# Thirty-one stores of a hybrid decoder layer issued from ScalarE's queue in place of SP's

## The chip, the cores and the metric

The kernel runs on one core of a Trainium2 chip. The core has five engines that run side by side, each with its own queue of instructions, executed in order: TensorE (PE: matrix products; PEld is its loading of weights), VectorE (DVE), ScalarE (ACT), GpSimd (POOL) and SyncE (SP), which only issues transfers. Transfers (DMAs) move data between the chip's memory and the on-chip buffers; sixteen DMA engines carry them out after some engine's queue has issued them. The metric is the time of one execution on the device in microseconds (us). Three runs of the kernel before gave 1281.14, 1285.14 and 1290.57 us; the median is 1285.14.

## What is computed

One layer of a decoder with two token mixers over 1024 tokens of width 1024. In float32, cut to what matters:

```python
h = rmsnorm(x, norm_w) * (1 + scale) + shift          # shift, scale, gate from c
z_ssm, xbc, dt_raw, q, k, v, z_att, f_logit, g_logit = split(h @ w_in)
y_ssm = ssd_branch(z_ssm, xbc, dt_raw, ...)           # conv, chunked scan (16 heads, chunks of 128)
y_att = fox_branch(q, k, v, z_att, f_logit, b_f)      # causal attention, 8 heads, forget gates
g_ssm, g_att = split(sigmoid(g_logit + b_gate))
merged = g_ssm * (y_ssm @ w_proj_ssm) + g_att * (y_att @ w_proj_att)
out = rmsnorm(x + gate * (merged @ w_out), final_norm_w)
```

## The kernel before

Every product is made of three passes of a reduced-precision matrix product: each operand is split into a high part (a cast on ScalarE, line 102) and a low part (a subtraction on GpSimd or VectorE, line 103). Weights come in as pieces of 128 x 512 floats into one of four raw buffers (`wr`, loaded at lines 89, 462 and 579), and are split into `wh` and `wl`. A raw buffer is free again once its low part has been made.

The stages follow each other in the code:

- To about 160 us: adaLN, the normalised and transposed input `hh`/`hl`, the first three gate slabs, the first V slab (`v_slab(0)`, narrow matmuls at lines 140 to 142, which also gives dt and the forget logits), sums of the input for the pair products (`t_forms`, lines 440 to 444), and the chain for dt (lines 369 to 396).
- To about 545 us: the pairs of slabs (`c_pair`, matmuls at lines 495 to 497), each pair of the projection's 128-column slabs by seven products instead of eight. Each slab's result is evacuated into a buffer of the ring `ev` (four buffers of 128 x 1028 floats) and stored to DRAM scratch: gates (line 187), z (526), the convolved x (545). Between them stand sums of later weights (lines 579 to 594).
- To about 770 us: the scan (`ssd_half`, 32 chunk steps of four heads). Each step loads `ab` from a_scr (line 681), makes the decay matrix on ScalarE (683, 685), VectorE (686) and the split (`m`), transposes x (691), updates the carried state (711 to 717) and makes the outputs (728, 739 and 740, 741 to 744). To keep TensorE busy, three V slabs (lines 140 to 142) and seven slabs of q and k (lines 115 to 117, `qk_spill`) are put among the steps as fill; V is stored at line 350, q and k at line 194.
- To about 1070 us attention by heads, which reads V, q and k back; then the rest of the output products.

All transfers are issued from SP's queue. The order of each queue is not the order of the code: a scheduler of the framework places every instruction of the whole program by the durations that it assumes and by priorities (the scan's steps have a higher one than the fill). A store waits on its queue until the engine that writes its source has finished; what stands behind it on that queue waits with it. Eight semaphores go round for the completion of transfers: a transfer also waits for the one that last used its semaphore, which is the eighth before it.

The stores in question are made by `gate_out` (16 gates), `qk_out` (7 slabs of q and k) and the evacuation of `v_slab` (two stores for each of four slabs), each of 512 KB. In all three the data are written by ScalarE: a tanh (186), a scaled copy (193), a copy (346).

Of the kernel before, what the change touches and what calls it, by code (L numbers as in the profile page):

```python
# [32 lines left out]
S = 1024  # L33
# [36 lines left out]
def build(ctx, tc, t):  # L70
    nc = tc.nc
    V, A, G, PE, SP = nc.vector, nc.scalar, nc.gpsimd, nc.tensor, nc.sync
# [10 lines left out]
    def ev(name):  # L83
        return evp.tile([P, 1028], F32, tag="ev", bufs=4, name=name)
# [42 lines left out]
    def t_slab(srcs, n, xh, xl, evac, per=None):  # L127

        us = [unit(s, 2 * n) for s in srcs]
        per = per or 512 // n  # L130
        st = 512 // per
        for tb0 in range(0, 8, per):
            ps = mm_tile()
            for i in range(per):
                ts = slice((tb0 + i) * P, (tb0 + i + 1) * P)
                o = ps[:, i * st:i * st + n]
                for k in range(8):
                    hi, lo = us[k // 2]
                    cs = slice((k % 2) * n, (k % 2 + 1) * n)
                    PE.matmul(o, lhsT=xh[k][:, ts], rhs=hi[:, cs], start=(k == 0), stop=False)  # L140
                    PE.matmul(o, lhsT=xh[k][:, ts], rhs=lo[:, cs], start=False, stop=False)  # L141
                    PE.matmul(o, lhsT=xl[k][:, ts], rhs=hi[:, cs], start=False, stop=(k == 7))  # L142
            evac(tb0, ps.rearrange("p (i c) -> p i c", i=per))
# [21 lines left out]
    g_scr = [dram.tile([P, S], F32, name=f"g_scr{j}") for j in range(16)]  # L165
# [8 lines left out]
    qk_scr = {(n, h): dram.tile([P, S], F32, name=f"{n}_scr{h}") for n, h in SPILL + PSPILL}  # L174
    v_scr = [[dram.tile([P, 4, 256], F32, name=f"v_scr{j}_{g}") for g in range(2)] for j in range(4)]
# [6 lines left out]
    def gate_out(j):  # L182
        gt = ev("gt")

        def evac(hs, ps):
            A.activation(out=gt[:, hs], in_=ps, func=AF.Tanh, scale=0.5, bias=cols[:, R_BG + j:R_BG + j + 1])
        return evac, lambda: SP.dma_start(out=g_scr[j], in_=gt[:, :S])

    def qk_out(n, h):
        qt = ev("qt")  # L190

        def evac(hs, ps):
            A.activation(out=qt[:, hs], in_=ps, func=AF.Copy, scale=-QSCALE if n == "q" else 1.0)
        return evac, lambda: SP.dma_start(out=qk_scr[n, h], in_=qt[:, :S])

    def w_in(n, i, p):
        if (n, i, p) in ws_scr:
# [4 lines left out]
    with tc.tile_pool(name="st", bufs=1, side="right") as st, \  # L202
# [119 lines left out]
        for slab in FIRST:  # L322
            evac, store = gate_out(slab - G0)
            for hf in range(2):
                evac(slice(hf * 512, (hf + 1) * 512), ups[slab, hf])
            store()
# [6 lines left out]
    def gate_slab(j):  # L333
        evac, store = gate_out(j)
        c_slab(t["w_c"], G0 + j, hh, hl, evac)
        store()

    def v_slab(pair, dtf=None):
        vt = []

        def evac(tb, ps):
            per = ps.shape[1]
            g, i = tb // 4, tb % 4
            if i == 0:
                vt.append(ev("vt")[:, :1024].rearrange("p (i c) -> p i c", i=4))
            A.copy(out=vt[g][:, i:i + per, :], in_=ps[:, :, 0:256])
            if dtf is not None:
                V.tensor_copy(out=dtf[:, tb:tb + per, :], in_=ps[:, :, 256:280])  # L348
            if i + per == 4:
                SP.dma_start(out=v_scr[pair][g], in_=vt[g])  # L350

        if dtf is not None:
            with tc.issue_after(was["last"].ins):
                t_slab([t["w_v0"][u] for u in range(4)], 280, hh, hl, evac)
        else:
            t_slab([t["w_v"][pair - 1, u] for u in range(4)], 256, hh, hl, evac)
# [3 lines left out]
    with tc.tile_pool(name="pa", bufs=1, side="right") as pa, \  # L360
# [235 lines left out]
        def slab_out(s):  # L596
            if s < XB0:
                return silu_out(z_scr[s])
            if s < Q0:
                return conv_out(s - XB0)  # L600
            if s < ZA0:
                return qk_out(*(("q", s - Q0) if s < K0 else ("k", s - K0)))
            if s < G0:
                return silu_out(za_scr[s - ZA0])
            return gate_out(s - G0)
# [24 lines left out]
    with tc.tile_pool(name="sd", bufs=1, side="right") as sd, \  # L630
# [119 lines left out]
        def qk_spill(n, h):  # L750
            evac, store = qk_out(n, h)
            c_slab(t["w_c"], (Q0 if n == "q" else K0) + h, hh, hl, evac)
            store()
# [3 lines left out]
        for qd in range(4):  # L757
            st32, sn = sd.tile([P, 256], F32, tag="st32", bufs=1, name="st32"), None
            for hf in range(2):
# [7 lines left out]
                for i in range(2):  # L767
                    j = 2 * qd + i
# [472 lines left out]
```

## Time and profile before

| | |
|---|---|
| median of three runs | 1285.14 us |
| the profiled execution | 1286.09 us, of it the span of the program 1284.4 us |
| busy in the span: TensorE, VectorE, GpSimd, ScalarE | 1183.9, 963.1, 776.1, 594.8 us |
| share of the DMA engines' time that SP's queue took | 51.5% |

A trace has each instruction's start and duration on its engine. Where an engine stood idle before an instruction, the profile names what ended the idle time: the instruction (with its engine, tile and line) or the transfer that released it. The issue of a transfer by SP is shown with the time that the issue itself took; when its data have landed is a separate number. SP's waits are counted from the end of the instruction before.

### The profile page before, as it was taken

The numbers are of one execution on the slowest core, as the hardware profiler recorded it, in microseconds if no ns is written. First come the engines' busy times: TensorE is split into PE (matmuls) and PEld (weight loads), VectorE is DVE, ScalarE is ACT, GpSimd is POOL, SyncE is SP. The second block draws the span as 40 slices with busy tenths as digits, with TensorE's granted clock in tenths as the row PEclk, the third lists the DMA queues.
The fourth block names the chain that finished last, engine by engine and source line by source line (L and its number), as shares of the span: only waits on it lengthen the run. The fifth ranks groups of instructions, "written<-read, shape, count | busy, mean of one in ns | idle before, by whom it ended". The sixth has DMA issues, their size and how long they took to land. (4 is left out here: it accounts for less than half of the span.)

```text
span 1284.4 us, 18783 instructions
## 1 busy us (share of the span) xinstructions
PE 1183.9 (92%) x6206; PEld 988.8 (77%) x6206; DVE 963.1 (75%) x1618; ACT 594.8 (46%) x1194; POOL 776.1 (60%) x644
## 2 busy tenths in 40 slices
PE   4897899999978999999988999999999999999896
PEld 3686688777766788799778888888887787878685
DVE  6979767787799566348689764545667968999997
ACT  5443324242423232477667733444456553444354
POOL 3258465474755476448887966435446635587666
PEclk9998899998989999999999999999999999999999
DMA  8422443624556566654565558623236619766143
GB/s 346 158 100 98 160 123 124 213 64 167 188 185 216 175 211 228 223 177 148 188 200 163 173 191 296 210 87 116 74 127 210 201 55 328 224 188 193 52 116 145
DMA packets 104126, 219.70 MB, mean 171 GB/s; under 512 B 11818, under 2 KB 19420, under 8 KB 103004
## 3 DMA queue, kind: packets, MB, share of 16 engines
q1 hardware_dynamic: 104028, 218.50, 51.5%
q8 instruction: 49, 0.80, 0.3%
q14 instruction: 49, 0.40, 0.1%
HBM read 154.85 MB, written 63.61 MB: 170 GB/s over the span
## 5 line engine op out<-in xcount | busy, mean ns | idle before, releaser
L103 POOL TENSOR_TENSOR wl<-wr,wh 128x512 fp32r<-128x512 f32 (+1 forms) x188 | 281.5, 1508 | 135.7 <-ACT wh L102 130.7
L102 ACT CAST wh<-wr 128x512 fp32r<-128x512 f32 (+1 forms) x214 | 129.8, 618 | 158.4 <-DMA wr<-w_c 53.7
L103 POOL TENSOR_TENSOR sl<-sr,sh 128x512 fp32r<-128x512 f32 x57 | 91.0, 1603 | 78.8 <-ACT sh L102 65.7
L115 PE MATMUL mm<-hh,wh 128*128 128x512 f32 x288 | 115.9, 407 | 4.3 <-ACT wh L102 1.9
L116 PE MATMUL mm<-hl,wh 128*128 128x512 f32 x288 | 116.7, 405 | 3.0 <-DVE hl L307 3.0
L117 PE MATMUL mm<-hh,wl 128*128 128x512 f32 x288 | 116.3, 405 | 0.0
L102 ACT CAST sh<-sr 128x512 fp32r<-128x512 f32 x57 | 34.1, 619 | 96.6 <-DVE sr L478 77.0
L140 PE MATMUL mm<-wh,hh 128*128 128x256 f32 (+1 forms) x256 | 74.9, 294 | 3.8 <-DVE tmp L348 3.8
L141 PE MATMUL mm<-wl,hh 128*128 128x256 f32 (+1 forms) x256 | 74.8, 293 | 0.0
L142 PE MATMUL mm<-wh,hl 128*128 128x256 f32 (+1 forms) x256 | 74.4, 292 | 0.0
L1018 ACT ACTIVATE pr<-pr,sm 128x1024 f32<-128x1024 f32 (+3 forms) x64 | 49.9, 780 | 50.4 <-DVE sm L1017 42.4
L1021 POOL TENSOR_SCALAR pr<-pr,sm 128x1024 f32<-128x1024 f32 (+3 forms) x64 | 48.6, 762 | 34.7 <-DVE sm L1020 30.2
L1013 DVE CUSTOM_DVE_ANT_0 pr<-lg,fb 128x512 f32<-128x512 f32 (+1 forms) x96 | 51.5, 551 | 23.5 <-PE lg L1012 14.0
L115 PEld LDWEIGHTS mm<-hh,wh 128*128 128x128 f32 x288 | 55.1, 193 | 15.6 <-ACT wh L102 2.4
L116 PEld LDWEIGHTS mm<-hl,wh 128*128 128x128 f32 x288 | 55.3, 192 | 14.7 <-DVE hl L307 3.9
L1004 POOL TENSOR_SCALAR_AFFINE_SELECT fb<-fb 128x128 f32<-128x128 f32 x64 | 21.9, 344 | 72.1 <-DVE sm L1013 57.3
L117 PEld LDWEIGHTS mm<-hh,wl 128*128 128x128 f32 x288 | 55.2, 192 | 10.8
L1037 DVE TENSOR_TENSOR ptl<-tp,pth 128x512 fp32r<-128x512 f32 (+1 forms) x80 | 50.1, 632 | 15.9 <-ACT pth L1036 15.5
L1036 ACT CAST pth<-tp 128x512 fp32r<-128x512 f32 (+1 forms) x80 | 42.3, 543 | 41.5 <-PE tp L1033 32.4
L683 ACT ACTIVATE ab<-ab,acs 128x128 f32<-128x128 f32 x128 | 41.1, 391 | 31.7 <-DMA ab<-a_scr 28.1
L140 PEld LDWEIGHTS mm<-wh,hh 128*128 128x128 f32 x256 | 49.5, 194 | 4.7 <-DVE tmp L348 4.5
L103 POOL TENSOR_TENSOR m<-ab,m 128x512 fp32r<-128x512 f32 x32 | 46.7, 1462 | 7.1 <-ACT m L102 4.7
(393 smaller groups left out, 3972.6 us busy)
## 6 DMA issues: line engine op xcount, KB each, us to landing
wr<-w_c SPq DMA_DIRECT2D x116, 256.0 KB, 3.5
wa<-w_ada SPq DMA_DIRECT2D x8, 1024.0 KB, 11.4
g_scr<-gt SPq DMA_DIRECT2D x16, 512.0 KB, 4.0
ab<-a_scr SPq DMA_DIRECT2D x32, 256.0 KB, 3.7
gt<-g_scr SPq DMA_DIRECT2D x32, 256.0 KB, 3.0
wr<-w_ps SPq DMA_DIRECT2D x28, 256.0 KB, 2.9
wr<-w_pa SPq DMA_DIRECT2D x28, 256.0 KB, 3.1
wr<-so SPq DMA_DIRECT2D x28, 256.0 KB, 2.6
```

Of the source, the lines that this page charges most:

```text
L102: A.copy(out=hi[:, :n], in_=raw[:, :n])
L103: eng.tensor_tensor(out=lo[:, :n], in0=raw[:, :n], in1=f32(hi[:, :n]), op=ALU.subtract)
L115: PE.matmul(ps, lhsT=hi[:, cs], rhs=xh[k][:, hs], start=(k == 0), stop=False)
L116: PE.matmul(ps, lhsT=hi[:, cs], rhs=xl[k][:, hs], start=False, stop=False)
L117: PE.matmul(ps, lhsT=lo[:, cs], rhs=xh[k][:, hs], start=False, stop=(k == 7))
L140: PE.matmul(o, lhsT=xh[k][:, ts], rhs=hi[:, cs], start=(k == 0), stop=False)
L141: PE.matmul(o, lhsT=xh[k][:, ts], rhs=lo[:, cs], start=False, stop=False)
L142: PE.matmul(o, lhsT=xl[k][:, ts], rhs=hi[:, cs], start=False, stop=(k == 7))
L1013: V.tensor_tensor_reduce(out=pr[:, n0:n1], in0=lg[:, :n1 - n0], in1=fb[:, n0:n1], op0=ALU.add, op1=ALU.min, scale=1.0, scalar=BIG, accum_o ...
L1018: A.activation(out=pr[:, :n], in_=pr[:, :n], func=AF.Exp, scale=-1.0, bias=sm[:, 0:1], accum_out=sm[:, 1:2])
L1021: G.tensor_scalar(out=pr[:, :n], in0=pr[:, :n], scalar1=sm[:, 1:2], scalar2=0.5, op0=ALU.mult, op1=ALU.mult)
L1037: V.tensor_tensor(out=ptl[:, :w], in0=tp[:, :w], in1=f32(pth[:, :w]), op=ALU.subtract)
```

## The change

Three functions issue their store with ScalarE's handle `A` in place of SP's. Nothing else in the code is changed: the same transfers move the same data.

```diff
@@ gate_out @@
-        return evac, lambda: SP.dma_start(out=g_scr[j], in_=gt[:, :S])
+        return evac, lambda: A.dma_start(out=g_scr[j], in_=gt[:, :S])
@@ qk_out @@
-        return evac, lambda: SP.dma_start(out=qk_scr[n, h], in_=qt[:, :S])
+        return evac, lambda: A.dma_start(out=qk_scr[n, h], in_=qt[:, :S])
@@ v_slab @@
             if i + per == 4:
-                SP.dma_start(out=v_scr[pair][g], in_=vt[g])
+                A.dma_start(out=v_scr[pair][g], in_=vt[g])
```

That makes 16 + 7 + 8 = 31 stores. Since the scheduler places everything anew, the order of other instructions changes too, in two stretches: at about 80 to 160 us, and from 545 to about 790 us. After that all engines have their old order, but for two neighbouring loads on SP.

On SP, at about 54 to 85 us (`wr<-w_ps` are loads of weights, `g_scr` the stores of the first three gates):

```order
 L89 DMA wr<-w_c 128x512 x2
-L579 DMA wr<-w_ps 128x512
-L187 DMA g_scr_95<-gt 128x1024
-L579 DMA wr<-w_ps 128x512
-L187 DMA g_scr_96<-gt 128x1024
-L579 DMA wr<-w_ps 128x512
-L187 DMA g_scr_97<-gt 128x1024
-L579 DMA wr<-w_ps 128x512
+L579 DMA wr<-w_ps 128x512 x4
```

The stores are gone from among the loads, which keep their order.

On ScalarE, at about 125 to 132 us (`gt` is a gate, `sh` the high part of a sum of weights, `thb_1136` that of a sum of the input):

```order
 L102 CAST thb_1136<-pe 128x512
 L102 CAST wh<-wr 128x512
+L102 CAST sh<-sr 128x512
+L186 ACTIVATE gt<-mm,cols 128x512
 L102 CAST thb_1136<-pe 128x512
-L102 CAST sh<-sr 128x512
+L102 CAST wh<-wr 128x512
 L186 ACTIVATE gt<-mm,cols 128x512
-L102 CAST wh<-wr 128x512
-L186 ACTIVATE gt<-mm,cols 128x512
+L187 DMA g_scr_98<-gt 128x1024
```

The cast of the weights' sum and the first half of the gate now stand ahead of the second cast of the input's sum, and the gate's store stands behind its second half.

On TensorE in the scan, at about 640 us, up to the 19th of the 56 state products of line 739 (`mm` are fill matmuls of the slabs of q and k, `sp` and `xp` belong to the scan). Before:

```order
L116 MATMUL mm<-hl_244,wh 128x512
L117 MATMUL mm<-hh_236,wl 128x512
L115 MATMUL mm<-hh_237,wh 128x512
L116 MATMUL mm<-hl_245,wh 128x512
L117 MATMUL mm<-hh_237,wl 128x512
L115 MATMUL mm<-hh_238,wh 128x512
L691 MATMUL xp<-ident,xs 128x128 x2
L116 MATMUL mm<-hl_246,wh 128x512
L117 MATMUL mm<-hh_238,wl 128x512
L115 MATMUL mm<-hh_231,wh 128x512
L116 MATMUL mm<-hl_239,wh 128x512
L739 MATMUL sp<-ch_4634,sn 128x128
```

And now:

```order
L711 MATMUL sp<-xr,bt 128x256 x3
L117 MATMUL mm<-hh_235,wl 128x512
L115 MATMUL mm<-hh_236,wh 128x512
L116 MATMUL mm<-hl_244,wh 128x512
L117 MATMUL mm<-hh_236,wl 128x512
L728 MATMUL sp<-m_5401,xr 64x128 x8
L691 MATMUL xp<-ident,xs 128x128 x2
L728 MATMUL sp<-m_5401,xr 64x128 x4
L115 MATMUL mm<-hh_237,wh 128x512
L116 MATMUL mm<-hl_245,wh 128x512
L739 MATMUL sp<-ch_4634,sn 128x128
```

The same step of the scan now has fewer fill matmuls ahead of it: counted from the start of the program, 260 of the wide ones (128 x 512, lines 115 to 117) in place of 290, and as before 576 of the narrow ones (lines 140 to 142).

## Rows read from the trace of the kernel before

**Rows 1.** Busy time by stretch: stretch, length, each engine's busy time (instructions), clock, DMA.
```profile
0.00:160.00 160.00, 123.63 (x595) 100.61 (x596) 129.85 (x220) 68.90 (x120) 78.56 (x62) 0.95 0.48 173
160.00:545.00 385.00, 362.72 (x1524) 289.42 (x1523) 279.13 (x346) 130.31 (x224) 229.50 (x151) 0.96 0.53 176
545.00:770.00 225.00, 210.86 (x1595) 191.16 (x1594) 164.67 (x332) 153.37 (x377) 169.61 (x156) 0.98 0.57 177
630.00:660.00 30.00, 25.25 (x163) 21.09 (x161) 21.75 (x52) 18.91 (x48) 23.39 (x23) 0.94 0.60 180
690.00:720.00 30.00, 26.73 (x204) 24.48 (x202) 26.03 (x47) 20.90 (x51) 23.72 (x22) 0.94 0.60 169
```
The busy times stand in the order PE, PEld, DVE, ACT, POOL; the clock is a share of full speed, then come the DMA share and GB/s.

**Rows 2.** Waits of SP's queue: line, released by; us, times, longest.
```profile
SPq L89 <- POOL wl L103: 97.8, 55, 11.7
...
SPq L187 <- ACT gt L186: 40.9, 9, 27.1
...
SPq L350 <- ACT vt L346: 28.3, 5, 17.9
...
SPq L194 <- ACT qt L193: 6.0, 5, 1.9
```

**Rows 3.** Line 187 on SP: ns min/median/max, then us to landing.
```profile
L187 SPq DMA_DIRECT2D g_scr<-gt x16: 320/351/1417, 81.5 to 547.0; - x16
...
DMA to landing us min/median/max: 2.6/4.0/5.0
```

**Rows 4.** SP in order of time, 81 to 119 us: start, us, what.
```profile
81.50 0.33 SPq L187 DMA_DIRECT2D g_scr<-gt  x1
82.97 0.33 SPq L579 DMA_DIRECT2D wr<-w_ps  x1
...
116.77 0.33 SPq L350 DMA_DIRECT2D v_scr<-vt  x1
118.70 0.33 SPq L462 DMA_DIRECT2D wr<-w_c  x1
```

**Rows 5.** ScalarE in order of time at 130 us; brackets: idle, released by.
```profile
130.27 0.62 ACT L102 CAST sh<-sr 128x512 fp32r<-128x512 f32 x1 [3.02 <-DVE sr L480]
```

**Rows 6.** TensorE in order of time at 131 and 141 us.
```profile
131.53 0.50 PE L495 MATMUL mm<-thb,sh 128*128 128x512 f32 x1 [3.87 <-ACT gt L186]
...
141.36 0.43 PE L393 MATMUL pp<-tri,tmp 128*64 128x128 f32 x2 [2.21 <-DVE tmp L387]
```

**Rows 7.** TensorE's waits, 545 to 770 us: us, times, longest.
```profile
PE xp L691 <- DVE xd L700: 5.4, 4, 2.6
PE xp L691 <- DMA xs<-x_scr: 4.7, 5, 1.9
```

**Rows 8.** TensorE in order of time at 554 us.
```profile
553.99 0.33 PE L691 MATMUL xp<-ident,xs 128*128 128x128 f32 x1 [0.48 <-DMA xs<-x_scr]
```

**Rows 9.** SP in order of time at 688 us.
```profile
688.28 0.33 SPq L350 DMA_DIRECT2D v_scr<-vt  x1
688.70 0.38 SPq L681 DMA_DIRECT2D ab<-a_scr  x1
```

**Rows 10.** ScalarE in order of time at 596 and 694 us.
```profile
596.09 1.28 ACT L683 ACTIVATE ab<-ab,acs 128x128 f32<-128x128 f32 x4 [0.60 <-DMA ab<-a_scr]
...
693.67 1.28 ACT L683 ACTIVATE ab<-ab,acs 128x128 f32<-128x128 f32 x4 [1.46 <-DMA ab<-a_scr]
```

**Rows 11.** ScalarE's longest wait, 545 to 770 us: us, times, longest.
```profile
ACT ab L683 <- DMA ab<-a_scr: 28.1, 18, 3.8
```

**Rows 12.** TensorE in order of time at 640 us.
```profile
640.26 0.40 PE L115 MATMUL mm<-hh,wh 128*128 128x512 f32 x1
640.49 0.39 PE L116 MATMUL mm<-hl,wh 128*128 128x512 f32 x1
640.73 0.22 PE L739 MATMUL sp<-ch,sn 128*128 128x128 f32 x1
```

**Rows 13.** VectorE in order of time at 639 us.
```profile
639.39 0.41 DVE L741 TENSOR_TENSOR ys<-sp,eb 128x256 f32<-128x256 f32 x1
```

## Prediction

> **What bounds the kernel now.** I read the busy time by stretch first. The span has five stages: adaLN and the transformed input to 160 us, the projections by pairs to 545, the scan to 770, attention to 1070, and the rest. In [rows 1] TensorE is busy 362.7 of 385 us in the pair stage and 210.9 of 225 in the scan, so it is nearly the bound in both; before 160 us it has 36.4 us of holes while VectorE is busy 129.9 of 160. What can be won in a stage is what TensorE waits there, and for whom.
>
> Then the SP queue's own waits [rows 2]. Stores of the gates held the queue 40.9 us in 9 waits, those of V 28.3 in 5, those of q and k 6.0 in 5: 75.2 us in which the queue could issue nothing. This is what the change takes away, and it looks large. But SP is not a bound by itself: the question is whether a transfer that stood behind such a store was ready before the store was. So the third view is SP's issues in order of time, and the fourth TensorE's waits in the scan.
>
> **The change, part by part.**
>
> *The waits taken off SP.* The two longest are at 54 to 81.5 us (27.1) and 98.8 to 116.8 us (17.9). Behind the first stands a load of w_ps at 82.97, behind the second one of w_c at 118.70 [rows 4]: 1.5 and 1.9 us after the store, not right behind it. Each waits for a raw weight buffer, of which there are four, until GpSimd has split its last content; GpSimd's splits hold the queue far longer (97.8 us at line 89 alone, [rows 2]). I went through all 31 stores like this. Behind 21 of them the next issue comes 0.4 us or more after the store's end, on a release of its own; behind the other ten it follows at once, but those have lost two microseconds at most. So the 75.2 us shrink to nearly nothing. Before 545 us I take 0.
>
> *A new order of the first stage.* The scheduler also moves a few steps at 120 to 140 us: VectorE's sum at line 480 stands ahead of two other steps now, and ScalarE's cast that waits for it (3.02 us, [rows 5]) no longer holds the gate's tanh for so long, for which TensorE waits 3.87 us at 131.53 [rows 6]. By the durations of VectorE's rows the sum would end about 2.8 us earlier. It is not a gain: at 141.36 TensorE waits for line 387 [rows 6], the end of the same VectorE work, of which none is taken away. The hole only moves. 0.
>
> *Entry to the scan.* The last gate's store stands in SP just ahead of the first x loads of the scan and took 1.42 us (the longest of [rows 3]). TensorE waited 0.48 us for such a load at 553.99 [rows 8]; the other waits for x loads (4.7 us in 5, [rows 7]) stand behind other traffic. I take -0.5.
>
> *Loads right behind a store.* In the scan two loads of a_scr that ScalarE then waited for stand next after a store of V: that at 688.70, 0.42 us behind the store, cost ScalarE 1.46 us at 693.67; another of the kind cost 0.60 at 596.09 [rows 9, 10]. Without the store ahead both could come sooner: 0 to -2.1 us, where ScalarE waits 28.1 us for these loads in all [rows 11], so most of that wait has other causes (the buffer is free only after GpSimd's split). Half of ScalarE's gain, as TensorE has other work: -1.0.
>
> *The issues on ScalarE.* 31 stores now take ScalarE's time. 17 of them stand before the scan, where ScalarE is busy 130.3 of 385 us and 68.9 of 160: hidden; if the cover were gone, 17 x 0.35 = 6.0 us. 14 (one gate, six of V, seven of q and k) stand in the scan, where ScalarE is busy 153.4 of 225 us, 68% [rows 1], and every chunk passes through it several times. No row shows an issue on ScalarE. The nearest rows are the same stores on SP, 0.32 us shortest, 0.35 median, 1.42 longest [rows 3]. Ends: 0 and 14 x 1.42 = 19.9 us. I take the median, 14 x 0.35 = 4.9 us, and of it the share in which ScalarE has no idle time to give, 68%: +3.3.
>
> A store also waits for the transfer eight issues earlier, since eight completion semaphores go round. On ScalarE that means waiting for a load that SP issued, which would hold all casts behind it. By this profile's times each such predecessor was issued at least 5 us before ScalarE comes to the store, and the gates' stores, twice as large as most of them, land in 4.0 us in the median, 5.0 at most [rows 3]. I take 0; each microsecond that SP falls behind would be held on ScalarE too.
>
> *The new order of the scan.* This is the largest unknown. From 545 to 790 us the scheduler has reshuffled all engines; after that they run in the old order. TensorE's steps of the scan now stand earlier among the fill matmuls (V, q and k products that fill its holes). At the 19th state product the old order has 290 wide fill matmuls ahead of it, the new one 260; the narrow ones are the same 576. In the trace that step starts at 640.73, wide matmuls follow each other every 0.23 us [rows 12], and its last input was there at 639.80 [rows 13]. If the chain of the scan keeps its times, TensorE arrives 30 x 0.23 = 6.9 us earlier and stands until 639.8 anyway: 6.9 less the 0.9 it was late, 6.0 us of new idle time. The fill left over is done later, so nothing gives this back. If instead the chain speeds up because TensorE serves it sooner, it is 0. TensorE already waits for the chain here, 4.7 of 30 us at 630 to 660 [rows 1], which speaks for the upper end; but most steps there found TensorE one or two microseconds late, which speaks for the lower. Halfway: +3.0.
>
> **Sum.** 0 + 0 - 0.5 - 1.0 + 3.3 + 0 + 3.0 = +4.8 us. The profiled execution took 1286.1 us, 0.95 more than the median of the runs, 1285.1; so about 1290.9 for it, and 1290 for the median.
>
> **Rivals.**
>
> *The order's full price.* The chain keeps its times and all 6.0 us are lost: +7.8, 1293. For it: the hole at 630 to 660. Against it: TensorE's own lateness held the chain's buffers.
>
> *Faster: the scan stops starving TensorE.* With no store ahead of the loads, and TensorE early at each step, the chain keeps pace with the new order. Then the holes in the scan go, 225 - 210.9 = 14.1 us, and with them the two stretches at 630 to 660 and 690 to 720 where the granted clock is 0.94 on average [rows 1], 0.06 x 30 us each, 3.6: -17.7, or 1267. It passes 1% once 12.9 of these 17.7 are won. For it: 4.7 us of the holes are x loads. Against it: 5.4 us are waits for VectorE [rows 7], GpSimd is busy 169.6 of 225, and ScalarE gets more to do. [...] No run here shows a second queue yet.
>
> *Slower: ScalarE sets the pace of the scan.* If each of the 14 issues costs as much as the longest on SP, and the casts behind it hold the chain, it is +19.9: 1305. It passes 1% from 0.92 us each on. For it: ScalarE has only a third of its time free there. Against it: the median on SP is 0.35. [...]
>
> *No effect at all.* All moved work is hidden and the two orders are worth the same: 1285.
>
> **How the numbers follow.** About 1% is what a measurement of this kernel can tell from no change, 12.9 us: the borders are 1272 and 1298. Chances: my sum 0.45, the order's full price 0.22, no effect 0.05, faster 0.11, slower 0.17. The first three lie within 1%, 0.72. The range leaves out the far halves of the two outer cases: 1274 to 1303.
>
> **What would show it.** In the new profile, SP's waits at lines 187, 194 and 350 are gone and those for GpSimd's splits have grown; the loads at about 83 and 118.7 us come when they came; TensorE's hole at 131 is shorter and that before line 393 longer; ScalarE shows 31 issues of about 0.35 us; TensorE is busy less than 210 of the scan's 225 us or the scan ends some 5 us later, and everything after it is shifted by as much. I am wrong if issues on ScalarE take about a microsecond or wait for SP's transfers, if the loads of a_scr and x land so much sooner that TensorE's holes in the scan shrink, or if the first stages move by more than 2 us.

## The result: slower by half a per cent

The changed kernel took 1291.91 us (median of 20 runs, 1286.36 to 1298.09), the kernel before 1287.32 beside it: a ratio of 1.0047, interval 1.0033 to 1.0060. The medians lie 4.6 us apart; the ratio is 6.0 us at this length, 4.2 to 7.7 by its interval. The forecast was 4.8 us more. The size is right; the experiments show that the parts of the sum are not.

The profiled execution is the shortest of the twenty, with a span of 1284.6 us against 1284.4 before. The loss can't be seen in it as a whole; it has to be read by stage. Busy time by stretch of the changed kernel, columns as in [rows 1]:

```profile
0.00:160.00 160.00, 122.70 (x602) 98.82 (x603) 131.07 (x222) 70.49 (x123) 77.59 (x63) 0.97 0.48 173
160.00:545.00 385.00, 363.61 (x1558) 291.32 (x1557) 281.96 (x347) 133.50 (x226) 228.10 (x151) 0.97 0.53 179
545.00:770.00 225.00, 208.08 (x1553) 184.60 (x1551) 154.73 (x329) 149.19 (x373) 172.22 (x156) 0.99 0.54 172
```

The granted clock was 0.97 and 0.97 before the scan, where it had been 0.95 and 0.96: this execution had fewer stretches at a clock of 0.50 (30.7 us of them to 545 us, in place of 44.4), and came to the scan 4.8 us earlier. Then it lost them again. To measure the scan without its start I use three marks, the first transpose of TensorE (line 691), the last update of the carried state on VectorE (line 717) and the first product behind the scan (line 784). For each line: count, duration in ns, first and last start. Before:

```profile
L691 PE MATMUL xp<-ident,xs x64: 270/273/477, 554.0 to 736.7; 128*128 128x128 f32 x64
L717 DVE SCALAR_TENSOR_TENSOR st<-st,ed,sp x96: 263/280/302, 578.2 to 752.5; 64x64 f32<-64x64 f32 x96
L784 PE MATMUL sp<-ones,sacc x16: 166/250/250, 768.2 to 769.8; 128*128 128x1 f32 x16
```

And after:

```profile
L691 PE MATMUL xp<-ident,xs x64: 270/273/417, 549.2 to 734.0; 128*128 128x128 f32 x64
L717 DVE SCALAR_TENSOR_TENSOR st<-st,ed,sp x96: 263/279/303, 572.9 to 748.3; 64x64 f32<-64x64 f32 x96
L784 PE MATMUL sp<-ones,sacc x16: 164/250/250, 768.3 to 769.9; 128*128 128x1 f32 x16
```

The scan took 768.2 - 554.0 = 214.2 us and now takes 219.1. The last state update came 198.5 us after the first transpose, and now 199.1: the chain of the carried state is hardly later. But from there to the end TensorE had 15.7 us of work, and now has 20.0: 82 wide fill products where there were 65, and 17 at 0.23 us [rows 12] are 3.9 us. TensorE's waits in the scan show where that work was not done (released by; us, times, longest). Before, beside those for x in [rows 7]:

```profile
PE sp L739 <- POOL sn L103: 0.5, 1, 0.5
PE sp L728 <- DVE st L717: 0.3, 1, 0.3
```

And after:

```profile
PE sp L739 <- POOL sn L103: 5.5, 6, 1.6
PE sp L728 <- DVE st L717: 3.4, 2, 1.8
PE sp L711 <- DVE st L713: 2.2, 1, 2.2
PE xp L691 <- DMA xs<-x_scr: 2.1, 4, 0.7
PE xp L691 <- DVE xd L700: 1.9, 3, 0.6
```

The waits for x fell from 10.1 to 4.0 us. Waits for the carried state (`sn`, `st`), 0.8 us before, are now 11.1. TensorE comes to the steps earlier and stands for the state instead, while the fill that could have covered it stands behind the step. (How much of this is the order and how much the queue, the experiments tell.)

What the change does on the queues came as written. SP's waits for the stores are gone, and those for the splits of weights have grown, at line 89 from 97.8 [rows 2] to 127.7 us:

```profile
SPq L89 <- POOL wl L103: 127.7, 64, 11.7
SPq L579 <- POOL wl L103: 98.3, 30, 27.0
SPq L462 <- POOL wl L103: 74.9, 24, 16.7
```

The gates' stores on ScalarE (ns min/median/max), to be read against [rows 3]:

```profile
L187 ACTq DMA_DIRECT2D g_scr<-gt x16: 326/326/445, 79.7 to 539.0; - x16
...
DMA to landing us min/median/max: 2.6/3.8/6.5
```

### The profile page after: what moved, and what is told of

It reads as the page before. It is cut to its first block, busy times and chain, and to the rows that moved or that the text cites. A ratio compares the mean times of both kernels' runs of the same rounds, so it can differ in the third digit from the quotient of the medians.

```text
span 1284.6 us, 18749 instructions
## 1 busy us (share of the span) xinstructions
PE 1184.0 (92%) x6206; PEld 984.9 (77%) x6206; DVE 952.6 (74%) x1618; ACT 595.7 (46%) x1194; POOL 778.6 (61%) x644
## 5 line engine op out<-in xcount | busy, mean ns | idle before, releaser
L117 PEld LDWEIGHTS mm<-hh,wl 128*128 128x128 f32 x288 | 55.0, 191 | 11.1
L683 ACT ACTIVATE ab<-ab,acs 128x128 f32<-128x128 f32 x128 | 41.1, 391 | 36.6 <-DMA ab<-a_scr 32.8
L541 DVE SCALAR_TENSOR_TENSOR cv<-xp,cols,cv 128x1024 f32<-128x1024 f32 x30 | 49.9, 1687 | 0.0
## 6 DMA issues: line engine op xcount, KB each, us to landing
wa<-w_ada SPq DMA_DIRECT2D x8, 1024.0 KB, 11.4
```

Of the source, the lines that this page charges most:

```text
L117: PE.matmul(ps, lhsT=lo[:, cs], rhs=xh[k][:, hs], start=False, stop=(k == 7))
L541: V.scalar_tensor_tensor(out=v, in0=xp[:, i:i + S], scalar=cols[:, R_CW + 10 * i + j:R_CW + 10 * i + j + 1], in1=v, op0=ALU.mult, op1=ALU.add)
```

## The experiments

Most of them hold the order of issue of each engine, so that the queue and the order can be changed one without the other. A helper at the end of the program chains each engine's instructions, without waits, in an order taken from another kernel; stores that change their queue are left to the scheduler, which puts them where their data are ready. The two theories at the start: the new order costs the time (A), or the second queue does, by its issues on ScalarE or by transfers that land later (Q). The texts written ahead of the runs name others by letters of their own; each is explained there.

```diff
         build(ctx, tc, t)
+        in_order(tc)
...
+def in_order(tc):
+    """Chain each engine's instructions (numbers by engine, in order of issue) without waits."""
```

All results. The ratio is to runs of the kernel before beside it, with its interval. "Scan" is the time from the first transpose to line 784, "state" the time to the last state update, "left" the difference: what TensorE still has to do then. The last two columns are TensorE's waits for the carried state (`sn`, `st`) and for x (`xd`, `xs`). These five are us of one profiled execution.

| kernel | stores, order | ratio | scan | state | left | waits: state | waits: x |
|---|---|---|---|---|---|---|---|
| before | SP, old | 1 | 214.2 | 198.5 | 15.7 | 0.8 | 10.1 |
| x_act_oldorder | ScalarE, old | 1.0001 (0.9982 to 1.0019) | 216.1 | 200.4 | 15.7 | 3.1 | 7.9 |
| x_act_quarters | ScalarE in quarters, old | 1.0013 (0.9992 to 1.0033) | 214.8 | 199.1 | 15.7 | 3.8 | 8.8 |
| x_sp_neworder | SP, new | 1.0031 (1.0012 to 1.0050) | 218.8 | 198.7 | 20.1 | 8.0 | 6.2 |
| x_sp_neworder_2 | the same | 1.0035 (1.0018 to 1.0052) | 219.4 | 199.3 | 20.1 | 6.2 | 6.7 |
| x_sp_scanorder | SP, new from the scan on | 1.0029 (1.0012 to 1.0046) | 218.5 | 198.3 | 20.2 | 8.0 | 5.9 |
| changed | ScalarE, new | 1.0047 (1.0033 to 1.0060) | 219.1 | 199.1 | 20.0 | 11.1 | 4.0 |
| after_again | the same | 1.0051 (1.0031 to 1.0071) | 221.4 | 201.3 | 20.1 | 11.0 | 6.7 |
| after_3 | the same | 1.0054 (1.0034 to 1.0074) | 221.9 | 201.8 | 20.1 | 11.4 | 6.4 |
| x_act_one_sp | ScalarE but one, new | 1.0040 (1.0020 to 1.0060) | 220.6 | 200.4 | 20.2 | 9.2 | 5.7 |
| x_rest_new | SP; TensorE old, others new | 1.0075 (1.0063 to 1.0087) | 227.7 | 211.3 | 16.4 | 3.6 | 11.4 |
| x_new_filled | SP, new, fill forward | 1.0029 (1.0012 to 1.0047) | 219.9 | 203.8 | 16.1 | 4.1 | 3.5 |
| x_old_filled | SP, old, fill forward | 0.9985 (0.9968 to 1.0002) | 213.6 | 202.3 | 11.3 | 3.5 | 3.3 |
| x_old_filled_2 | the same | 0.9971 (0.9957 to 0.9985) | 211.8 | 200.5 | 11.3 | 2.0 | 4.4 |

**The change once more (after_again), and queue and order apart.** The second and third kernels undo one half each: `x_sp_neworder` is the kernel before with the changed kernel's order, `x_act_oldorder` the changed kernel with the order of before. `x_sp_scanorder` has the new order from the scan on alone.

> The changed kernel once more, for a second profile. Its first profile ends the pair stage 4.8 us earlier than the kernel before and then takes 4.9 us longer for the scan (from the first transpose of line 691 to the first product of line 784: 219.1 us in place of 214.2). Theory A (the scan's new order costs about 5 us; what came earlier was the granted clock of one execution, which differs from run to run): the scan takes 218 to 220 us again, the pair stage ends anywhere between 537 and 543 us, and the time is 1.003 to 1.006 of before. Theory B (the change really gains 3 to 5 us before the scan, and loses more later): the pair stage ends at about 537 us again.

> All 31 stores back on SP, but every other instruction on all engines held in the changed kernel's order. Theory A (order): as slow as the changed kernel, 1.003 to 1.006 of before, the scan 218 to 220 us. Theory Q (the issues on ScalarE, or transfers of a second queue that land later, cost it): no difference from before, 0.999 to 1.001, the scan 214 us. If both count: about 1.002.

> All 31 stores on ScalarE, but every other instruction on all engines held in the order of the kernel before. Theory A (order): no difference from before, 0.999 to 1.001, the scan 213.5 to 215 us. Theory Q (queue): as slow as the changed kernel, 1.003 to 1.006. My prediction's own split (issues +3.3, loads -1.5): 1.001 to 1.002.

> All stores on SP, the order of the kernel before up to 350 us and the changed kernel's order from there on, which is the scan's. Theory A: the scan's order alone has the whole price, 1.003 to 1.006 of before. If the new order of the first stage (before 160 us) has a part in it: less than with the new order everywhere, by that part; if that first-stage order is a gain, more.

Theory A held. The order alone costs 0.3%, the queue alone nothing that can be told in the old order (its interval reaches to 0.2% either way); the new order of the first stage adds nothing that can be told to the scan's (1.0029 and 1.0031). The column "left" separates cleanly: 15.7 us in every run with the old order on all engines, 20.0 to 20.2 in every run with the new one, whichever queue the stores are on. These 4.4 us are the price of the order; in the time, 0.29 to 0.35%, it is 3.7 to 4.5 us. The waits of the table show 2.0 to 3.3 us of it (10.9 us before for state and x together, 12.9 to 14.2 with the new order on SP); where TensorE spent the rest is not shown. The gain of 4.8 us ahead of the scan was one execution's: the three profiles of the changed kernel begin the scan at 549.2, 554.8 and 552.6 us, the kernel before at 554.0, so theory B fell.

After_again's scan was 221.4 us, above the 218 to 220 expected: with the new order the queue seems to cost something after all.

**The price of an issue on ScalarE.** Each store in four quarters, in the old order:

```diff
-        return evac, lambda: A.dma_start(out=g_scr[j], in_=gt[:, :S])
+        return evac, lambda: quarters(A, g_scr[j], gt)
...
+def quarters(eng, scr, src):
+    for c in range(0, S, S // 4):
+        APART.append(eng.dma_start(out=scr[:, c:c + S // 4], in_=src[:, c:c + S // 4]).ins.name)
```

> All stores on ScalarE in four quarters each (124 issues in place of 31, 56 in place of 14 in the scan; the same bytes), every other instruction in the order of the kernel before. The prediction's rule for an issue in the scan (0.35 us times the 68% in which ScalarE is busy): 42 more of them cost 10 us over the run with whole stores, 1.008. Theory H (an issue lies beside the work ScalarE's datapath is doing already, and the next instruction starts at most 0.2 us later): under 2 us, 1.000 to 1.0015.

1.0013, the scan 214.8 us: some 40 more issues in the scan cost nothing that can be told, and the interval (to 1.0033) leaves out the 1.008 of the prediction's rule. Theory H held, and ScalarE's rows in order of time show why. A store of k of the changed kernel:

```profile
651.31 0.39 ACT L102 CAST xr<-xd 128x256 fp32r<-128x256 f32 x1
651.44 0.35 ACTq L194 DMA_DIRECT2D k_scr<-qt  x1
651.61 0.62 ACT L102 CAST m<-ab 128x512 fp32r<-128x512 f32 x1
```

The issue begins while the cast ahead of it still runs, and the next cast starts 0.30 us after the first. Without a store between them the same two casts, in the run with quarters, also stand 0.30 us apart:

```profile
642.46 0.40 ACT L102 CAST xr<-xd 128x256 fp32r<-128x256 f32 x1
642.76 0.61 ACT L102 CAST m<-ab 128x512 fp32r<-128x512 f32 x1
```

The 0.35 us lie beside ScalarE's own work, unless the store stands right behind the instruction that writes its data (at 730.22 us in the changed kernel ScalarE stands 0.45 us there) or the issue is long. Four of the 124 issues in the run with quarters took 0.73 to 1.79 us; ScalarE stood until the longest had ended:

```profile
604.67 1.79 ACTq L1208 DMA_DIRECT2D v_scr<-vt  x1
606.51 0.63 ACT L685 ACTIVATE ab<-ab 128x512 f32<-128x512 f32 x1 [0.82 <-ACT sn L102]
```

Why it was long is not shown. The scan as a whole lost nothing by it that can be told.

**Which engines' order it is.** With stores on SP, only TensorE goes back to its old order:

> Stores on SP; from the scan on VectorE, ScalarE, GpSimd and SP keep the changed kernel's order, TensorE alone goes back to the order of the kernel before, so 290 wide fill products stand ahead of the 19th state product again. Theory P (the price of the new order is TensorE coming to the steps 3 to 6 us of fill too early and then standing for the carried state): most of it goes, 0.999 to 1.001, waits for the state (sn, st) back from 8 us to under 3. Theory R (the price lies in the order of the other engines, which make the state later): 1.002 to 1.004 or more, and the waits stay.

Neither theory. The waits for the state did go back, to 3.6 us, and "left" to 16.4, as theory P said; but the time rose to 1.0075. Now TensorE stands ahead of the transposes of x (line 691) for 16.8 us. Its waits in the scan ("issue": the profile shows nothing that it waited for):

```profile
PE xp L691 <- DVE xd L700: 7.7, 6, 2.9
PE xp L691 <- issue: 5.4, 2, 4.0
PE xp L691 <- DMA xs<-x_scr: 3.7, 5, 1.3
```

TensorE's order and that of the others belong together: this mixture delays the state itself, by 13 us. The run can't say which engine's order has the price.

**The changed kernel against its order on SP, again.**

> The changed kernel's order with all stores on SP, once more, beside the next one: it was 1.0031 of before. Theory A alone (order): the same as the changed kernel. Theory A with a queue's price in the new order: 1.5 to 3 us less than the changed kernel.

> The changed kernel a third time, on the same chip as the run before it. By its earlier medians 1.0045 to 1.0055 of before; if order is all, 1.003 like the run before it. The scan takes 218 to 222 us, of which TensorE waits 8 to 11 us for the carried state.

1.0035 and 1.0054 on one chip, as 1.0031 and 1.0051 were: in both pairs the stores on ScalarE cost 0.2%, by the medians 1.7 and 3.1 us. Each interval by itself reaches to the other's ratio. The profiles point the same way: "state" is 198.3 to 199.3 us in three runs with the new order on SP, and 199.1, 201.3 and 201.8 in three with it on ScalarE, and the longest landing of a load of a_scr is 6.0 to 6.7 us in the three on SP, 7.8 to 7.9 in the three on ScalarE. So in the new order the queue probably delays the chain, by some 2 us. That this needs the new order is not shown: in the old one the longest landing rose as well, from 5.3 us to 8.5, and "state" from 198.5 to 200.4, with an interval of the time that would hide 2 us; with the stores in quarters they were 6.0 us and 199.1.

**One store back on SP.** TensorE's wait for `st` at line 711 showed one place where the two differ in every profile.

```diff
-                A.dma_start(out=v_scr[pair][g], in_=vt[g])
+                (SP if (pair, g) == (3, 1) else A).dma_start(out=v_scr[pair][g], in_=vt[g])
```

> The changed kernel with one of its 31 stores back on SP: the V store at about 611 us, which is issued within 0.05 us of a load of a_scr and so travels beside it. In all three profiles of the changed kernel TensorE waits 2.15 to 2.18 us ahead of the 25th state update (line 711), in the three with the same order and all stores on SP 0.94 to 0.97. If the transfer beside the load makes this difference: 0.9 to 1.1 us here, and the load of a_scr is used 3.4 us after its issue in place of 3.9 to 4.0. If not: 2.2 us again. In the time it is about 1 us, less than can be told.

It came as the first case. The changed kernel, from SP's, ScalarE's, VectorE's and TensorE's rows in order of time (brackets: idle, released by):

```profile
610.67 0.33 SPq L681 DMA_DIRECT2D ab<-a_scr  x1
610.72 0.33 ACTq L350 DMA_DIRECT2D v_scr<-vt  x1
614.65 1.28 ACT L683 ACTIVATE ab<-ab,acs 128x128 f32<-128x128 f32 x4 [3.44 <-DMA ab<-a_scr]
616.70 1.73 DVE L686 TENSOR_TENSOR ab<-ab,cb 128x512 f32<-128x512 f32 x1 [5.21 <-POOL wl L103]
618.90 0.59 PE L711 MATMUL sp<-xr,bt 128*128 128x256 f32 x3 [2.18 <-DVE st L713]
```

And with this store on SP, behind the load:

```profile
614.57 0.33 SPq L681 DMA_DIRECT2D ab<-a_scr  x1
614.99 0.38 SPq L350 DMA_DIRECT2D v_scr<-vt  x1
618.10 1.28 ACT L683 ACTIVATE ab<-ab,acs 128x128 f32<-128x128 f32 x4 [3.00 <-DMA ab<-a_scr]
620.15 0.98 DVE L686 TENSOR_TENSOR ab<-ab,cb 128x512 f32<-128x512 f32 x1 [4.76 <-ACT ab L685]
621.61 0.59 PE L711 MATMUL sp<-xr,bt 128*128 128x256 f32 x3 [0.97 <-DVE st L713]
```

The load that travels beside a store is used 3.98 us after its issue (3.87 and 4.35 in the two other profiles of the changed kernel), the load ahead of the store after 3.53. That half microsecond became 1.2 since VectorE's product at line 686 then took 1.73 us in place of 0.98. This shows one place where the queue costs a wait; the others I have not taken apart. In the time it can't be told: 1.0040, where the changed kernel had 1.0047 to 1.0054.

**Fill moved forward.** If the time is lost where TensorE stands and fill remains for later, fill should be put where it stands. Only TensorE's order differs here, from that of the kernel before in `x_old_filled` and from that of `x_sp_neworder` in `x_new_filled`.

> Stores on SP and the order of the kernel before on all engines, except that in the scan fill matmuls are moved forward on TensorE, each to a place where the trace of the kernel before shows TensorE standing ahead of a step, and only if their weights were ready by then. No step of the scan gets more work ahead of it than it waits for. Theory P (the scan's time is what TensorE waits at its steps, and where the fill lies sets that wait): with the chain's times kept, 7.0 us of the 13.7 us of holes are left and the scan is 4.4 us shorter: 0.9966 of before, faster by about 0.3%. Theory C (the chain of the scan on VectorE, ScalarE and GpSimd sets the time, and steps only wait longer elsewhere): 0.999 to 1.001.

> Stores on SP and the changed kernel's order, except that fill matmuls are moved forward on TensorE in the same way, to where the run x_sp_neworder shows it standing. That run was 1.0031 to 1.0035 of before. Theory P: 4.0 us less, so 1.000 to 1.001; the waits for the carried state fall from 8 us to under 4. Theory C: 1.003 again, the waits move to other steps.

> The kernel before with fill moved forward in the scan, once more, since its first interval (0.9968 to 1.0002) just holds 1. Theory P: 0.997 to 0.999 again, TensorE's holes in the scan about 10 us in place of 13.7. Theory C: 1.000. In its first profile TensorE ran 10.2 us at half clock from 699 us on, where the fill had run out; if that comes again, it is what keeps the gain under the 4.4 us that were worked out.

In both orders "left" fell as planned, by 4.4 and 4.0 us, but the state paid some of it back. In the old order 1.9 and 3.7 us of gain remained: 0.9985 and 0.9971. The first interval just holds 1, the second does not: this version is 0.2 to 0.3% under the kernel before, and the changed kernel is 0.5% above it. In the new order the state came 5 us later and the gain was gone: theory C by the time. TensorE stood for weights of fill that was taken too early, as its rows in order of time show:

```profile
664.11 0.58 PE L140 MATMUL mm<-wh,hh 128*128 128x256 f32 x1 [2.43 <-ACT wh L102]
```

Behind this wait, and where the fill had run out (no fill product in the 11 us from 704.5 on), the clock fell. Busy time by stretch of `x_new_filled`:

```profile
655.00:675.00 20.00, 16.45 (x119) 15.17 (x117) 11.67 (x26) 11.04 (x29) 12.67 (x14) 0.83 0.45 132
700.00:725.00 25.00, 19.86 (x119) 16.09 (x118) 23.07 (x41) 19.39 (x47) 22.04 (x20) 0.80 0.64 213
```

At 0.83 of 20 us and 0.80 of 25 that is 3.4 + 5.0 = 8.4 us of clock lost, which is an upper bound of the time, since TensorE was not busy throughout. The second profile of `x_old_filled` has the same at 690 to 720:

```profile
690.00:720.00 30.00, 25.53 (x157) 21.10 (x157) 26.70 (x43) 21.72 (x55) 23.73 (x22) 0.83 0.53 168
```

0.17 x 30 = 5.1 us, where the kernel before lost 0.06 x 30 = 1.8 in that stretch [rows 1]: 3.3 us more by the same bound, enough for the 2.0 us by which the state came later in that execution.

## Why the prediction was right, and where its parts were not

*SP's waits: 0.* Right. The load behind the first long wait came at 81.16 us in place of 82.97 [rows 4], which is no more than the 1.8 us by which TensorE's work around it was early as well. The one at 118.70 came at 112.83, 4 us sooner than that shift, which I had excluded; but the next load moved only with the rest, from 120.08 to 118.29, and nothing gained by it. The old order with the stores on ScalarE is at 1.0001. SP in order of time:

```profile
81.16 0.33 SPq L579 DMA_DIRECT2D wr<-w_ps  x1
...
112.83 0.33 SPq L462 DMA_DIRECT2D wr<-w_c  x1
...
118.29 0.33 SPq L462 DMA_DIRECT2D wr<-w_c  x1
```

*The first stage: the hole only moves, 0.* Right. In place of 3.87 and 2.21 us [rows 6], TensorE in order of time:

```profile
135.20 0.50 PE L495 MATMUL mm<-thb,sh 128*128 128x512 f32 x1 [1.88 <-ACT pe L503]
139.44 0.69 PE L393 MATMUL pp<-tri,tmp 128*64 128x128 f32 x2 [3.51 <-DVE tmp L387]
```

*Entry to the scan, -0.5, and loads right behind a store, -1.0.* Wrong: neither gain came. TensorE's wait for the first load of x, 0.48 us before [rows 8], was 0.38, 0.71 and 1.19 in the three profiles of the changed kernel. ScalarE's wait for a_scr did not fall but rose from 28.1 [rows 11] to 32.8 us (35.5 and 36.7 in the other two profiles):

```profile
ACT ab L683 <- DMA ab<-a_scr: 32.8, 20, 4.3
```

Most of that rise comes with the new order, and not with the queue. In `x_sp_neworder`, with the stores on SP (33.8 and 34.3 in the two other runs of that kind):

```profile
ACT ab L683 <- DMA ab<-a_scr: 31.4, 20, 3.2
```

What the queue adds is the later landing. A store on another queue does not stand ahead of a load any more; it travels beside it, and in the one place taken apart, where the two are issued 0.05 us from each other, the load was used 3.98 us after its issue in place of 3.53. That is 0.45 us later, as much as the 0.42 us that the issue would have saved. I had counted only what the load gains.

*Issues on ScalarE, +3.3.* Wrong: nothing that can be told. The duration was right (0.326 us median; I had 0.35), the share in which it counts was not. I took ScalarE's busy share, 68%, as the part of an issue that costs; most issues ran beside ScalarE's work, and four times as many did not show in the time. Where SP and ScalarE issue within 0.05 us of each other, at 610.67 and 610.72, both take 0.33, and no issue of the changed kernel on ScalarE took more than 0.45; why four in quarters took longer is not shown. The wait for the transfer eight issues earlier cost nothing, as I had taken: in the trace of the kernel before the 724 transfers do take eight semaphores in turn, but the 22 waits for a semaphore that stand on ScalarE's queue ahead of these stores in the changed kernel took 17 ns each.

*The new order of the scan, +3.0 (0 to 6.0).* The mechanism is the one named: TensorE early at the steps, new idle time, the fill left for later. The size was too small by 1.4 us: 4.4 in the scan, 0.29 to 0.35% in the time, 3.7 to 4.5 us. The place was wrong: the 19th state product has no wait; the 21st, 25th and 27th wait 0.94, 1.62 and 1.31 us. And that nothing gives the fill back was wrong: the 30 wide products missing ahead of the 19th are 9 ahead of the 23rd (308 in place of 317), and 17 at the end of the chain. The deficit at one step is not the price; what is left at the end is. That the middle was taken for want of a reason is what failed here; the row that speaks for the upper end (holes at 630 to 660) was the better one.

*The sum.* The order was set 1.4 us too low and the issues 3.3 too high; the first load of x and the loads behind a store were counted as -1.5 where the queue costs probably about +2. Put right, the sum is 4.4 + 2 = 6.4 us, against 4.6 by the medians and 6.0 by the ratio (6.6 and 7.0 by the ratios of the two repeats). The total came out because errors of both signs met, which is luck. Of the rivals the order's full price comes nearest; that ScalarE sets the pace is out by the quarters, and the faster case failed on its own condition: waits for x did shrink, with the stores on SP too, but the chain did not keep pace. The range was also not what its reason says: 1274 leaves out the whole of the faster case (1267 to 1272), and not its far half.

## What to carry to other kernels

A scheduler that places a whole program anew makes a change of queue a change of order; compare the orders first, and price where the bound engine will stand and what it has left when the chain ends. A second queue took 75.2 us of waits for stores off the first here, but transfers that followed each other then travel side by side, which in the one place taken apart made a load 0.45 us later (3.98 us in place of 3.53): look at which critical load would get a neighbour. One profile is one execution: the same kernel came to the scan 5.6 us apart in two executions, with a granted clock of 0.97 and 0.96 in the stretch before, so measure a stage from marks inside it.

## What the runs showed of the hardware that I had not expected

- The issue of a transfer on ScalarE (0.35 us at 651.44) leaves the distance of the casts around it unchanged, 0.30 us; an issue of 1.79 us made ScalarE stand for 0.82.
- VectorE's product at line 686, which reads two tiles, took 1.73 us when it started at 616.70, just behind a split of weights on GpSimd, and 0.98 when it started at 620.15, ahead of it. The split took 1.27 us in the changed kernel and 1.73 with the store on SP:

```profile
616.61 1.27 POOL L103 TENSOR_TENSOR wl<-wr,wh 128x512 fp32r<-128x512 f32 x1
```

```profile
620.54 1.73 POOL L103 TENSOR_TENSOR wl<-wr,wh 128x512 fp32r<-128x512 f32 x1
```

So in these rows the one that starts second is the longer one: the product 1.73 us in place of 0.98, the split 1.73 in place of 1.27. (In the second profile of the changed kernel the two start within 0.02 us of each other, and the product takes 1.83.) Why is not shown, nor that it is always so: at 631.20 in the changed kernel the product starts 0.16 us behind a split and takes 0.68. Here it turns 0.45 us of a late load into 1.2 us of a late step.
- Less idle time in the scan did not all come back as time: with fill moved forward (`x_old_filled_2`) no fill product starts in the 9 us after 697 us, TensorE was busy 25.5 us of the 30 from 690 us on (26.7 before), and the clock granted there was 0.83 on average, where it had been 0.94.
